# A feed-forward down projection computed by block products: seven 2x2 products in place of eight, with the sums of the activations formed one stage earlier

## The chip, the cores and the metric

One core of a Trainium2 chip runs the whole program. The metric is device time in microseconds (us), the median of several executions, lower being better. The engines are TensorE (PE; its weight loads are listed apart as PEld), VectorE (DVE), ScalarE (ACT), GpSimd (POOL) and SyncE (SP), whose queue issues all DMAs here.

## The reference, cut

One decoder layer over 1024 prompt tokens and 64 sample tokens (8 sequences of 8), width D = 1024, feed-forward width 3072. The change concerns the last third of it, the feed-forward block and the final norm:

```python
h = modulate(x, p['g_norm2'], sh2, sc2)
up = h @ p['w_up']                               # 1024 -> 6144
uc, new_ffn_conv = causal_dwconv(ffn_conv, up, p['ffn_conv_w'], p['ffn_conv_b'])
ua, ub = jnp.split(uc, 2, axis=-1)
x = x + gt2[:, None] * ((jax.nn.gelu(ua) * ub) @ p['w_down'])   # 3072 -> 1024
...
y = rmsnorm(x, g_final)
```

All inputs and outputs are float32. TensorE runs on rounded float32 ("fp32r"), so each product is made of three matmuls: high part by high part, high by low, low by high. Splitting a tile in two costs one ACT copy (high part) and one DVE subtraction (low part).

## The kernel before, in words

Channels lie on the 128 partitions, tokens along the free axis. Tokens come in two halves: half 0 holds the 64 sample tokens and 512 prompt tokens (576 columns, multiplied as two pieces of 288), half 1 holds 512 prompt tokens. `x2d` in DRAM holds the residual, `modT` the gates.

**The up stage** (`up`, L1458) already uses seven block products for eight. For each of 24 blocks of 256 output channels (12 steps `b`, two parts each: the gelu side, then the other) a `Quad` (L1296) makes 2x2 blocks of output: two output channel groups by two token halves, from K cut in two. The products are `p1`, `p5`, `p6`, `p2`, `p3`, `p7` of one Quad and `p4` of the one before, which `up` places behind `p1`. `prod` (L1236) makes each of four channel blocks by three matmuls; of kind "w" with two 288-column pieces (p1, p2, p4, p6), "e" with 512 columns (p3, p5), "p" with two pieces of 256 (p7). `Blocks` (L1253) loads four weight blocks, forms four sums (`sums`, on DVE), and `take` splits one into a ring of 3 pairs `wh`, `wl`. Raw blocks and sums share `WR` = 9 buffers (tag "wr"), copies of partial results 4 buffers (tag "cp").

`evac_up` (L1390) brings a block of output from PSUM to SBUF, `finish` (L1474) applies the convolution (`conv_up`: one ACT and two DVE instructions), the gelu, and in part 1 the product with the gelu side (L1490), and stores the result to `actd` in DRAM (L1489, L1491): six DMAs per step.

**The down stage** then closes the pools of the up stage and opens its own, loads half 0's 24 activation blocks through 3 staging buffers (`load_act`, L1494) and splits each. `down_a` (L1502) makes 4 strips (`strip`, L211) of 256 output channels for half 0: 24 blocks of K x 2 groups x 3 matmuls x 2 pieces. `down_b` (L1521) loads half 1 and makes the same for it, 24 x 8 x 3 products: 468 matmuls of 512 columns and, for the last six blocks of K in three of the strips, 216 of 256 columns, so that the first 256 tokens are finished while the others are still being multiplied. Each strip of half 1 ends in a residual update kept in SBUF, squares for the norm, and `final` (L1578), which makes the norm from matmuls with a matrix of ones (`rstd_from`, L353), a square root on ACT and a reciprocal on DVE (L368), and multiplies and stores `y`. `final` of half 0 runs under half 1's matmuls.

The order on each engine is set at build time by the framework's scheduler: instructions whose inputs are expected to be there go first by program order, and `tc.high_priority` moves some ahead. On the chip each queue then keeps that order. A tile of a pool with n buffers waits until the tile n places earlier is released.

Of the kernel before, what the change touches and what calls it, by code (L numbers as in the profile page):

```python
# [42 lines left out]
NOUT = _n  # L43
# [8 lines left out]
def _body(ctx, nc, tc, a):  # L52
# [36 lines left out]
    obuf = const.tile([128, NOUT], F32, name="obuf")  # L89
# [68 lines left out]
    def rg(name):  # L158
        return tmp("rg", [128, 604], name, bufs=5 if two else 7)
# [985 lines left out]
    WR = 9  # L1145
# [61 lines left out]
    def h2b(ST):  # L1207
# [23 lines left out]
        for j in range(4):  # L1231
            c = load("xc", 2 * j + 1, 3)
            V.tensor_sub(A[j], c, A[j])
            split_form(form("T4", j), A[j])

    def prod(acc, kind, wt, n, start=False, stop=False):  # L1236
        hi, lo = [x.rearrange("p (j c) -> p j c", c=128) for x in wt]
        for j in range(4):
            X = F[n, j]
            for i, (y, r) in enumerate(((hi, 0), (hi, 1), (lo, 0))):  # L1240
                f = dict(start=start and j + i == 0, stop=stop and j == 3 and i == 2, skip_group_check=True)
# [11 lines left out]
    class Blocks:  # L1253


        def __init__(self, w, own=()):
            self.w, self.t = w, dict(own)

        def load(self, *names):
            for n in names:  # L1260
                t = self.t.setdefault(n, None)
                if t is None:
                    t = self.t[n] = wt("wr", f"w{n}", F32, WR)
                nc.sync.dma_start(t, self.w[{"A11": 0, "A12": 1, "A21": 2, "A22": 3}[n]])

        def sums(self, eng):
            t = self.t
            t["S1"] = wt("wr", "S1", F32, WR)
            eng.tensor_add(t["S1"], t["A21"], t["A22"])
            t["S2"] = wt("wr", "S2", F32, WR)  # L1270
# [3 lines left out]
            t["S4"] = wt("wr", "S4", F32, WR)  # L1274
            eng.tensor_sub(t["S4"], t["A12"], t["S2"])

        def take(self, n):
            with tc.high_priority(offset=300):
                hi, lo = wt("wh", "wh", F32R, 3), wt("wl", "wl", F32R, 3)
# [6 lines left out]
    def blocks_of(w):  # L1286
        q = Blocks(w)
# [5 lines left out]
    def product(q, acc, kind, n, x, **f):  # L1293
        prod(acc, kind, q.take(n), x, **f)

    class Quad:  # L1296


        def __init__(self, q, evac):
            self.q, self.evac, self.p3_ = q, evac, None  # L1300
# [5 lines left out]
        def p1(self):  # L1306
            self.b = mm("b")
            product(self.q, self.b, "w", "A11", "B11", start=True, stop=True)
            self.t1 = tmp("cp", [128, 576], "t1", bufs=4)
            self.cp(halves(self.t1), self.b[:, :, :288])  # L1310

        def p2(self):
            a_ = mm("a")
            product(self.q, a_, "w", "A12", "B21", start=True, stop=True)
            self.evac(0, 0, a_[:, :, :288], halves(self.t1))

        def p3_first(self, e):
            self.e = e
            product(self.q, e, "e", "S4", "B22", start=True, stop=True)
            self.p3_ = tmp("cp", [128, 576], "p3", bufs=4)[:, :512]  # L1320
            self.cp(self.p3_, e)

        def p5_last(self):
            product(self.q, self.e, "e", "S1", "T1", stop=True)
# [490 lines left out]
```

## Time and profile before

| | |
|---|---|
| median of 3 runs | 1755.53 us (1755.03 to 1757.67) |
| the profiled execution | 1756.53 us |
| its span, first to last instruction | 1754.7 us |
| matmuls busy, share of the span | 97% |
| VectorE, ScalarE busy | 71%, 52% |
| last matmul of the up stage ends | 1432.5 us into the span |
| last matmul of the down stage ends | 1743.5 us into the span |

Times inside the execution are counted from the start of its span. An idle time in square brackets is that of the engine just before the instruction, with the instruction that ended it. Matmuls overlap, so a single one's duration is longer than its share of a run of them.

### The profile page before, as it was taken

The page shows a single profiled execution, that of the slowest core. Times are in us where ns is not written, and L with a number is a line of the kernel's source. Part 1 is how long each engine was busy: PE and PEld are TensorE (multiplying, and loading weights), DVE is VectorE, ACT ScalarE, POOL GpSimd, SP SyncE. Part 2 cuts the span into 40 slices and gives each one's busy share as a digit, 9 for nine tenths or more (in the row PEclk, how much of TensorE's full clock was granted, in tenths as well). Part 3 has the DMA queues.
Part 4 walks back from the last instruction along what each step waited for, and adds up shares of the span by engine and source line. Part 5 has one row for each costly group of instructions (what it writes and reads, how often), then busy time and mean ns, then how long its engine had stood idle before and what let it go on. Part 6 is the DMA issues. An engine that isn't in the chain of part 4 may idle for free.

```text
span 1754.7 us, 29379 instructions
## 1 busy us (share of the span) xinstructions
PE 1698.0 (97%) x10542; PEld 1531.1 (87%) x10542; DVE 1241.7 (71%) x2629; ACT 913.7 (52%) x1608; POOL 219.6 (13%) x488
## 2 busy tenths in 40 slices
PE   7999999999999999999997999999999979999997
PEld 3899999999997877888776999999999968999887
DVE  8878688967846788666759877777777755436426
ACT  4557758535535587744446555555555544224224
POOL 0012110100000001020021222222222220000000
PEclk9999999999999999999999999999999989999999
DMA  8275334366646655445672222222222238546634
GB/s 304 77 228 180 101 107 137 119 187 207 194 139 199 206 182 153 124 156 183 202 232 71 78 74 74 75 74 74 78 79 83 70 99 260 163 128 189 200 93 137
DMA packets 151826, 250.87 MB, mean 143 GB/s; under 512 B 34048, under 2 KB 43264, under 8 KB 151680
## 3 DMA queue, kind: packets, MB, share of 16 engines
q1 hardware_dynamic: 151680, 248.99, 45.6%
q8 instruction: 83, 1.36, 0.3%
q14 instruction: 63, 0.52, 0.1%
HBM read 205.20 MB, written 43.73 MB: 142 GB/s over the span
## 4 chain that ended last, share of the span: by engine, by line
PE 69%; DVE 5%; DMA 4%; ACT 2%; issue 1%; POOL 0%; SPq 0%; POOLq 0%; DVEq 0%; ACTq 0%
PE mm L226 16%; PE b L1248 13%; PE mm L224 12%; PE e L1244 7%; PE mm L1536 7%; PE a L1248 4%; PE b L1251 3%; DMA al<-act 2%; DMA xB<-x 1%; PE pv L787 1%; PE pg L961 1%; DVE wlo L179 1%; PE sada L274 1%; PE sada L273 1%; DMA tgb<-tg 0%
## 5 line engine op out<-in xcount | busy, mean ns | idle before, releaser
L179 DVE TENSOR_TENSOR wlo<-raw,whi 128x512 fp32r<-128x512 f32 x310 | 214.1, 691 | 208.1 <-ACT whi L178 178.7
L178 ACT ACTIVATE whi<-raw 128x512 fp32r<-128x512 f32 x310 | 194.4, 628 | 315.9 <-PE mm L224 107.7
L224 PE MATMUL mm<-h1A,whi 128*128 128x288 f32 x1024 | 183.3, 298 | 0.0
L226 PE MATMUL mm<-h1B,whi 128*128 128x512 f32 x512 | 159.9, 393 | 0.0
L224 PEld LDWEIGHTS mm<-h1A,whi 128*128 128x128 f32 x1024 | 151.3, 189 | 0.2
L1248 PE MATMUL b<-T,wh 128*128 128x288 f32 x768 | 134.8, 297 | 7.9 <-ACT gl L1482 6.1
L1248 PEld LDWEIGHTS b<-T,wh 128*128 128x128 f32 x768 | 115.3, 190 | 10.7 <-ACT gl L1482 6.3
L245 ACT ACTIVATE wh<-wA 128x512 fp32r<-128x512 f32 x94 | 59.2, 630 | 109.7 <-PE b L1248 42.6
L226 PEld LDWEIGHTS mm<-h1B,whi 128*128 128x128 f32 x512 | 95.6, 188 | 23.1
L224 PE MATMUL mm<-h1A,wlo 128*128 128x288 f32 x512 | 110.6, 297 | 2.0 <-DVE wlo L179 2.0
L226 PE MATMUL mm<-h1B,wlo 128*128 128x512 f32 x256 | 100.7, 393 | 0.7 <-DVE wlo L179 0.7
L224 PE MATMUL mm<-act,whi 128*128 128x288 f32 x512 | 91.9, 300 | 2.0 <-ACT act L1157 1.0
L1383 DVE SCALAR_TENSOR_TENSOR uc<-up,vec,uc 128x624 f32<-128x624 f32 (+1 forms) x96 | 76.0, 806 | 22.2 <-POOL up L1375 12.4
L1383 DVE SCALAR_TENSOR_TENSOR gl<-up,vec,gl 128x624 f32<-128x624 f32 (+1 forms) x96 | 75.9, 805 | 20.5 <-ACT gl L1381 15.0
L224 PEld LDWEIGHTS mm<-h1A,wlo 128*128 128x128 f32 x512 | 82.4, 189 | 2.3 <-DVE wlo L179 2.3
L246 DVE TENSOR_TENSOR wl<-wA,wh 128x512 fp32r<-128x512 f32 x94 | 64.9, 691 | 26.8 <-ACT wh L245 26.3
L1248 PE MATMUL b<-T,wl 128*128 128x288 f32 x384 | 82.7, 297 | 0.0
L1536 PE MATMUL mm<-act,whi 128*128 128x512 f32 (+1 forms) x304 | 82.7, 359 | 0.0
L224 PEld LDWEIGHTS mm<-act,whi 128*128 128x128 f32 x512 | 76.6, 191 | 3.7 <-DVE act L1158 2.1
L245 ACT ACTIVATE wh<-S 128x512 fp32r<-128x512 f32 x72 | 45.0, 625 | 58.7 <-PE b L1248 42.6
L224 PE MATMUL mm<-act,w 128*128 128x288 f32 x384 | 56.5, 302 | 12.7 <-ACT act L1157 11.4
L1248 PE MATMUL b<-B,wh 128*128 128x288 f32 x384 | 67.2, 296 | 0.0
(456 smaller groups left out, 4370.5 us busy)
## 6 DMA issues: line engine op xcount, KB each, us to landing
raw<-w_in SPq DMA_DIRECT2D x128, 256.0 KB, 2.8
raw<-w_down SPq DMA_DIRECT2D x105, 256.0 KB, 2.8
wA<-w_up SPq DMA_DIRECT2D x94, 256.0 KB, 2.7
raw<-w_ada SPq DMA_DIRECT2D x56, 256.0 KB, 3.1
act<-uc SPq DMA_DIRECT2D x48, 256.0 KB, 2.1
araw<-w_ada SPq DMA_DIRECT2D x20, 512.0 KB, 7.0
s5a<-s5d SPq DMA_DIRECT2D x16, 512.0 KB, 3.8
raw<-w_rgp SPq DMA_DIRECT2D x32, 256.0 KB, 2.7
```

The source lines that it names most:

```text
L178: S.activation(hi, raw, AF.Copy)
L179: V.tensor_sub(lo, raw, hi.bitcast(F32))
L224: T_.matmul(T[m][:, h, :288], y[:, k, c], x[:, r, h * 288:(h + 1) * 288], **f)
L226: T_.matmul(T[0][:, m, tok], y[:, k, c], x[:, r, tok], **f)
L245: S.activation(hi, src, AF.Copy)
L246: V.tensor_sub(lo, src, hi.bitcast(F32))
L273: T_.matmul(sa[:18], csr[:, kb], hi, start=kb == 0, stop=False)
L1244: T_.matmul(acc, w, x, **f)
L1248: T_.matmul(acc[:, h, :288], w, x[:, h * 288:(h + 1) * 288], **f)
L1251: T_.matmul(acc[:, h, o:o + 256], w, x[:, h * 256:(h + 1) * 256], **f)
L1383: V.scalar_tensor_tensor(dst, t[:, k:k + n], fw[:, k, m:m + 1], dst, op0=OP.mult, op1=OP.add)
L1536: T_.matmul(T[:, m, tok], y[:, k, c], act[kb][:, r, tok], start=kb + n == 0, stop=kb == 23 and n == 2, skip_group_check=True)
```

## The change

The down projection becomes 16 Quads: four passes `ch`, each over three of the twelve pairs of activation blocks, times four groups of 256 output channels. Each Quad makes seven products of three channel blocks (w_down blocks of 128x384). Both token halves are made together. The sum of a pass goes into the residual in DRAM (`x2d` is read and written in every pass; in the last pass the result stays in SBUF). The seven activation forms of a pair (B11, B21, B22 and the sums T1 to T4) are formed in `finish` and stored in DRAM, 84 blocks in all in place of 48; the down stage loads and splits each once, with 28 buffers for 21 forms of a pass. `final` runs for half 1 behind the last Quad's p7 and for half 0 behind its p4. The weight buffers "wr" (now 8) and "cp" (now 5, in the same pool) live through both stages and also stage the forms; "uc" has 4 buffers for 3, "cs" 3 for 2; `obuf` moves to another pool; in `up_lead` the first Quad's p5 comes before the second's p3.

```diff
-    obuf = const.tile([128, NOUT], F32, name="obuf")
+    obuf = ph.tile([128, NOUT], F32, name="obuf")
...
-        return tmp("rg", [128, 604], name, bufs=5 if two else 7)
+        return tmp("rg", [128, 604], name, bufs=3 if two else 7)
...
+    ORDER, WIDE = ("B11", "T1", "T2", "B21", "B22", "T3", "T4"), ("B11", "B21", "T2", "T4")
-    actd = [dp.tile([24, 128, WID[h]], F32, name=f"act{h}") for h in range(2)]
+    actd = {n: dp.tile([12, 128, 576 if n in WIDE else 512], F32, name=f"act{n}") for n in ORDER}
...
-    WR = 9
+    WR = 8
...
-        for j in range(4):
-            X = F[n, j]
+        for j, X in enumerate(forms):
...
+    def cpt(name):
+        return uw.tile([128, 576], F32, tag="cp", name=name, bufs=5)
...
+        Q[0].p5_last()
         Q[1].p3_first(e[:, 1])
-        for q in Q:
-            q.p5_last()
+        Q[1].p5_last()
...
-            u, g = tmp("xc", [128, 632], "uc", bufs=3), gl[i, half]
+            u, g = tmp("xc", [128, 632], "uc", bufs=4), gl[i, half]
             conv_up(t, m, u[:, :n])
             if half == 0:
-                c = tmp("cs", [128, 64], "cs", bufs=2)
+                c = gl["c", i] = tmp("cs", [128, 64], "cs", bufs=3)
                 G.tensor_mul(two4(s8(c)), useg(u), useg(g))
-                nc.sync.dma_start(actd[0][k][:, :64], c)
-            V.tensor_mul(u[:, :512], u[:, :512], g[:, :512])
-            nc.sync.dma_start(actd[half][k][:, 512 * half - 512:] if half else actd[0][k][:, 64:576], u[:, :512])
...
+            u = gl["u", i, half] = u[:, :512]
+            V.tensor_mul(u, u, g[:, :512])
+        if part == 0:
+            return
+        b = k // 2
+        x = [gl["u", i, h] for h in range(2)]
+        if i == 0:
+            t1 = gl["T1"] = gl[0, 1][:, :512]
+            V.tensor_sub(t1, x[1], x[0])
+            store("B11", b, x[0], gl["c", 0])
+            store("T1", b, t1)
+            return
+        t2, t3, t4 = gl[0, 0][:, :512], gl["u", 0, 1], gl[1, 0][:, :512]
+        V.tensor_sub(t2, x[1], gl["T1"])
+        V.tensor_sub(t3, x[1], t3)
+        V.tensor_sub(t4, x[0], t2)
+        c = tmp("cs", [128, 64], "cs", bufs=3)
+        G.tensor_sub(c, gl["c", 1], gl["c", 0])
+        store("B21", b, x[0], gl["c", 1])
+        store("B22", b, x[1])
+        store("T2", b, t2, gl["c", 0])
+        store("T3", b, t3)
+        store("T4", b, t4, c)
+
+    def store(n, b, x, c=None):
+        d = actd[n][b]
+        if c is None:
+            nc.sync.dma_start(d, x)
+            return
+        nc.sync.dma_start(d[:, 32:544], x)
+        for h in range(2):
+            nc.sync.dma_start(d[:, 544 * h:544 * h + 32], c[:, 32 * h:32 * h + 32])
...
+        def load(ch, names):
+            for n in names:
+                for p in range(3 * ch, 3 * ch + 3):
+                    w = 576 if n in WIDE else 512
+                    x = FD[n, p] = pp.tile([128, 2, 576], F32R, tag="act", name=f"{n}_{p}", bufs=28)[:, :, :w]
+                    t = cpt("f") if n in WIDE else wt("wr", "f", F32, WR)
+                    nc.sync.dma_start(t, actd[n][p])
+                    split_form(x, t)
...
+            def evac(i, half, y, z):
+                m = 2 * b + i
+                d = x2d[half][m * 128:(m + 1) * 128]
+                if ch < 3:
+                    x = tmp("xr", [128, 512], "xr", bufs=5)
...
+                nc.sync.dma_start(x, d)
+                with tc.high_priority(offset=400):
+                    if z is None:
+                        z = cpt("c21")
+                        S.activation(halves(z), y, AF.Copy)
+                    else:
+                        o = halves(z) if len(y.shape) == 3 else z
+                        V.tensor_add(o, y, o)
+                if half == 0:
+                    t = tmp("rs", [128, 64], "rs")
+                    G.tensor_mul(two4(s8(t)), sv(z), two4(bc(modT[:, 40 + m, 1:9], [128, 8, 8])))
+                    G.tensor_add(xs[:, m], xs[:, m], t)
+                    z = z[:, 32:544]
+                V.scalar_tensor_tensor(x, z, modT[:, 40 + m, 0:1], x, op0=OP.mult, op1=OP.add)
+                if ch < 3:
+                    nc.sync.dma_start(d, x)
+                elif b < 3:
+                    acc_sq(acc[half], x, m == 0)
+                    S.activation(x, x, AF.Copy, scale=v("gf")[:, m:m + 1])
+                else:
+                    last[half].append(rg("sq")[:, :512])
+                    S.activation(last[half][-1], x, AF.Square)
...
+        load(0, ORDER)
+        for ch in range(4):
+            for b in range(4):
+                q = Quad(blocks_of(a["w_down"][b, ch], 384), evac_down(ch, b),
+                         lambda n, ch=ch: [FD[n, p] for p in range(3 * ch, 3 * ch + 3)])
+                q.p1()
+                if pend is not None:
+                    pend.p4()
+                ahead = (lambda n: load(ch + 1, (n,))) if ch < 3 and b == 3 else lambda n: None
+                if ch < 3 and b == 2:
+                    load(ch + 1, ORDER[:2])
+                q.p5()
+                ahead("T2")
+                q.p6()
+                ahead("B21")
+                q.p2()
+                ahead("B22")
+                q.p3()
+                ahead("T3")
+                q.p7()
+                ahead("T4")
+                pend = q
+        final(1, acc[1], last[1], X3[1])
+        pend.p4()
+        final(0, acc[0], last[0], X3[0])
+
+    def final(half, acc3, sq, X):
+        r = rstd_from([acc3, *sq], 512, "rstdF", f"rstdF{half}")
+        gf = v("gf")
...
-    early.close()
     pairs.close()
...
-    wp, tp, ph = pool("w2", 2), pool("tmp2", 2), pool("part2")
     pp = pool("act")
+    tp = pool("tmp2", 2)
     two = True
-    down_a()
-    down_b()
+    down()
...
-    A["w_down"] = blocks(f("w_down")[0])
+    w = f("w_down")[0].reshape(4, 3, 2, 128, 4, 2, 128)
+    A["w_down"] = np.ascontiguousarray(w.transpose(4, 0, 5, 2, 3, 1, 6)).reshape(4, 4, 4, 128, 384)
```

## Rows read from the trace of the kernel before

**Rows 1.** The page's engine table: busy time, share of the span, instructions.

```profile
PE 1698.0 (97%) x10542; PEld 1531.1 (87%) x10542; DVE 1241.7 (71%) x2629; ACT 913.7 (52%) x1608; POOL 219.6 (13%) x488
```

**Rows 2.** Chain of work, one Quad of the up stage: start us, us, engine, line, count.

```profile
1215.39 6.40 PE b L1248 x48
1221.80 2.80 PE e L1244 x12
1224.59 3.20 PE b L1248 x24
1227.80 3.20 PE a L1248 x24
1230.99 2.79 PE e L1244 x12
1233.79 2.84 PE b L1251 x24
```

**Rows 3.** Timeline of PE: end of up, start of down, end of down.

```profile
1432.09 0.42 PE L1248 MATMUL b<-T,wl 128*128 128x288 f32 x2
1443.57 4.99 PE L224 MATMUL mm<-act,w 128*128 128x288 f32 x24 [11.06 <-ACT act L1157]
...
1743.22 0.28 PE L1536 MATMUL mm<-act,wlo 128*128 128x256 f32 x1
```

**Rows 4.** Busy us (count) of PE, PEld, DVE, ACT, POOL; PEclk, DMA share, GB/s.

```profile
1102.50:1145.00 42.50, 42.50 (x291) 40.35 (x290) 32.97 (x49) 21.79 (x34) 11.53 (x30) 1.00 0.25 77
...
1440.00:1450.00 10.00, 6.34 (x32) 5.79 (x32) 4.67 (x7) 4.92 (x9) 0.00 (x0) 0.66 0.84 278
...
1490.00:1500.00 10.00, 9.37 (x71) 9.16 (x70) 7.10 (x16) 5.25 (x9) 0.00 (x0) 1.00 0.93 299
...
1580.00:1600.00 20.00, 20.00 (x152) 20.00 (x152) 12.10 (x19) 10.63 (x19) 0.00 (x0) 1.00 0.77 242
```

**Rows 5.** Timeline of DVE, ACT and SP around a store in a step of up.

```profile
1272.16 0.68 DVE L1490 TENSOR_TENSOR uc<-uc,gl 128x512 f32<-128x512 f32 x1
...
1274.98 0.91 ACT L1381 ACTIVATE gl<-up,vec 128x624 f32<-128x624 f32 x1 [1.12 <-POOL up L1371]
...
1286.82 1.62 ACT L1381 ACTIVATE gl<-up,vec 128x624 f32<-128x624 f32 x2 [0.33 <-POOL up L1371]
...
1259.08 0.33 SPq L1489 DMA_DIRECT2D act<-cs  x1
```

**Rows 6.** Groups by line and shape, DVE in up: busy us, mean ns, idle before.

```profile
L246 DVE TENSOR_TENSOR wl<-wA,wh 128x512 fp32r<-128x512 f32 x64 | 43.9, 685 | 16.8 <-ACT wh L245 16.4
L1383 DVE SCALAR_TENSOR_TENSOR uc<-up,vec,uc 128x512 f32<-128x512 f32 x32 | 23.9, 746 | 0.6
L1405 DVE TENSOR_TENSOR up<-a,t 128x576 f32<-128x576 f32 x16 | 12.1, 758 | 19.7 <-PE a L1248 19.7
```

**Rows 7.** A tile's instructions: min/median/max ns of a 256-column split on DVE.

```profile
L246 DVE TENSOR_TENSOR gw<-e,gw x16: 410/418/428, 137.8 to 736.2; 128x256 fp32r<-128x256 f32 x16
```

**Rows 8.** Groups by line and shape, DVE in down.

```profile
L1158 DVE TENSOR_TENSOR act<-al,act 128x512 fp32r<-128x512 f32 x24 | 16.5, 690 | 14.6 <-ACT act L1157 14.4
L1158 DVE TENSOR_TENSOR act<-al,act 128x576 fp32r<-128x576 f32 x5 | 3.8, 759 | 4.6 <-ACT act L1157 4.6
L368 DVE RECIPROCAL rstdF<-sd 128x512 f32<-128x512 f32 x1 | 3.4, 3354 | 1.3 <-ACT sd L363 1.3
```

**Rows 9.** DMA totals of two stretches: 1440 to 1490, then 1480 to 1500.

```profile
DMA packets 6933, 13.35 MB, mean 267 GB/s; under 512 B 771, under 2 KB 771, under 8 KB 6929
...
DMA packets 3198, 5.97 MB, mean 299 GB/s; under 512 B 351, under 2 KB 351, under 8 KB 3197
```

**Rows 10.** Timeline: a norm's matmuls and square root, and DVE's last work.

```profile
902.17 1.98 PE L357 MATMUL prs<-sq,ones 128*128 128x512 f32 x4
...
904.19 0.69 ACT L363 ACTIVATE rstdB<-prs,epst 128x512 f32<-128x512 f32 x1
...
1748.60 2.77 DVE L1593 TENSOR_TENSOR x<-x,rstdF 128x256 f32<-128x256 f32 x8
```

More of the change, by code (lines that the diff above doesn't have):

```diff
@@ L1253, in _body, with __init__ @@
     class Blocks:
-        def __init__(self, w, own=()):
-            self.w, self.t = w, dict(own)
+        def __init__(self, w, own=(), n=512):
+            self.w, self.t, self.n = w, dict(own), n
         def load(self, *names):
@@ L1291, in blocks_of, with __init__, prod @@
         return q
-    def product(q, acc, kind, n, x, **f):
-        prod(acc, kind, q.take(n), x, **f)
     class Quad:
-        def __init__(self, q, evac):
-            self.q, self.evac, self.p3_ = q, evac, None
+        def __init__(self, q, evac, forms):
+            self.q, self.evac, self.F, self.p3_ = q, evac, forms, None
+        def prod(self, acc, kind, w, x, **f):
+            prod(acc, kind, self.q.take(w), self.F(x), **f)
         def cp(self, dst, src):
@@ L1307, in p1 @@
             self.b = mm("b")
-            product(self.q, self.b, "w", "A11", "B11", start=True, stop=True)
-            self.t1 = tmp("cp", [128, 576], "t1", bufs=4)
+            self.prod(self.b, "w", "A11", "B11", start=True, stop=True)
+            self.t1 = cpt("t1")
             self.cp(halves(self.t1), self.b[:, :, :288])
@@ L1313, in p2 @@
             a_ = mm("a")
-            product(self.q, a_, "w", "A12", "B21", start=True, stop=True)
-            self.evac(0, 0, a_[:, :, :288], halves(self.t1))
+            self.prod(a_, "w", "A12", "B21", start=True, stop=True)
+            self.evac(0, 0, a_[:, :, :288], self.t1)
         def p3_first(self, e):
             self.e = e
-            product(self.q, e, "e", "S4", "B22", start=True, stop=True)
-            self.p3_ = tmp("cp", [128, 576], "p3", bufs=4)[:, :512]
+            self.prod(e, "e", "S4", "B22", start=True, stop=True)
+            self.p3_ = cpt("p3")[:, :512]
             self.cp(self.p3_, e)
         def p5_last(self):
-            product(self.q, self.e, "e", "S1", "T1", stop=True)
+            self.prod(self.e, "e", "S1", "T1", stop=True)
         def c12(self):
@@ L1388, in useg, with up_forms @@
         return two4(seg(x, 546, 10)[:, :, :8])
+    def up_forms(n):
+        return [F[n, j] for j in range(4)]
     def evac_up(b, part, gl):
@@ L1396, in evac @@
             o = t[:, 32:544] if half else t[:, :576]
-            o = halves(o) if len(y.shape) == 3 else o
+            o, z, e = [halves(x) if len(y.shape) == 3 and x is not None else x for x in (o, z, e)]
             with tc.high_priority(offset=400):
@@ L1462, in up @@
             for part in range(2):
-                q = Quad(blocks_of(a["w_up"][12 * part + b]), evac_up(b, part, gl))
+                q = Quad(blocks_of(a["w_up"][12 * part + b]), evac_up(b, part, gl), up_forms)
                 q.p1()
```

159 lines of the change are left out of this document (41 added, 118 removed).

## The prediction, made before the changed kernel was run

> **What bounds the kernel now.** I read the page's engine table first: PE is busy for 97% of the span [rows 1], so what shortens the matmuls shortens the kernel, unless another engine or the DMAs take over. Then the chain of waits through the up stage, because it holds the very Quad that the change brings to the down stage. One Quad is six entries of PE with nothing between them [rows 2]: 6.40 + 2.80 + 3.20 + 3.20 + 2.79 + 2.84 = 21.23 us. So a Quad with four channel blocks per product can run at PE's pace, with DVE busy for 33.0 and ACT for 21.8 us of the 42.5 us of a step (two Quads) and DMA at 77 GB/s [rows 4]. Last, PE's timeline at the seams [rows 3]: the up stage's last matmul ends at 1432.5, the first of the down stage comes at 1443.6 after 11.06 us idle, the last ends at 1743.5, and the span at 1754.7. The down stage's matmuls thus lie in 311.0 us, and 11.2 us of norm and store follow.
>
> **Part 1, the products (removed and added).** Prices per matmul come from the runs in rows 2: 3.20/24 = 0.133 us for 288 columns, 2.80/12 = 0.233 for 512, 2.84/24 = 0.118 for 256. Before: half 0 has 24 x 8 x 3 x 2 = 1152 of 288 columns, 153.6 us; half 1 has 468 of 512, 109.2, and 216 of 256, 25.6. Sum 288.4 us. After: a Quad with three channel blocks costs 21.23 x 9/12 = 15.92 us, and 16 of them 254.8 us. **Gain 33.6 us**, all on the path. That is 11.6%, not the eighth that the count of products promises, because four of the seven carry the wider half of the tokens and p7 goes in pieces of 256.
>
> **Part 2, the seam between up and down.** Of the 311.0 us before, 311.0 - 288.4 = 22.6 us were lost, nearly all at the start: the 11.06 us until weights and activations arrive through newly opened pools, PE at its lower clock just after (granted clock 0.66 over 1440 to 1450, 24 matmuls in 4.99 us instead of 3.2), and a first strip that waits for each activation block [rows 3, 4]. After, the weight pool stays open, so the first Quad's weights are split before the up stage ends, and B11 can be staged early, since pass 0 needs only pairs stored long ago. But the forms take the place of the up stage's, and the four T4 tiles of up are read until its very last product. Right after it DVE has to finish the up stage (four convolution steps of 0.75, two products and three new sums of 0.69, about 6.5 us), and T2 and B21 stand behind that: p6 of the first Quad would like them 2.4 + 2.1 = 4.5 us after 1432.5. I price this at 9 us of lost PE, two or three waits and the lower clock after them. Bounds: 3 us if the splits find gaps, 17 us if each of B21, B22, T3 and T4 waits for a staging buffer (five "cp" buffers for 12 wide forms beside the Quad's own three). **Gain 13.6 us** (5.6 to 19.6).
>
> **Part 3, inside the down stage.** DVE: a split or sum of 384 columns lies between 0.418 for 256 [rows 7] and 0.685 for 512 [rows 6], so 0.55 us. A Quad has 7 splits and 4 sums (6.1), three additions from PSUM of at most 0.76 (2.1) and four residual updates of 0.746 (3.0): 11.2 us of 15.92. A pass adds 12 wide form splits of 0.759 and 9 of 0.690 [rows 8], 15.3 us: 60.1 of 63.7 us by durations, 94%. Eight instructions of 0.418 take 2.77 us [rows 7, 10], so each is worth some 0.07 less, and the pass comes to 53.5 us, 84%, as in a step of up with its new sums. But the forms bunch. Seven of the 28 buffers are free ahead; the other 14 forms can be split only while the last Quad of a pass gives up the old ones: 11.2 + 14 x 0.73 less the overlap is about 19 us of DVE in 15.9. The forms are due between 7 and 18 us into the next pass, so most of this is paid from slack. DMA: a pass moves 16 weight blocks of 197 KB, 5.9 MB of forms, and reads and writes 4.2 MB of residual each, 17.5 MB in 63.7 us. Over the first three passes, with the first and last pass's forms, it is 56 MB in 191 us, **293 GB/s**. Where queues were full the trace shows 267 and 299 GB/s [rows 9], and at 299 PE ran 9.4 of 10 us [rows 4]. At 299 the three passes are bound by PE, at 267 they take 210 us, 19 more. My terms for seam and passes, 9 + 9 = 18 us over 191, amount to the same as the lower rate, which is the row with the same mix of staged loads. So I take **3 us of stall at each of three changes of pass, loss 9 us** (0 to 27). ACT has less to do than DVE in every stretch of rows 4 and is given nothing of its own.
>
> On DMA size the Trainium skill speaks against the change ("DMA: Bandwidth & Descriptors", Bandwidth): it asks for at least 1 MiB per DMA for three quarters of the peak, and gives 138 GB/s at 64 KB and 341 at 1 MB. The new DMAs are 192 to 288 KB, so by interpolation, an estimate from that page, they would move well under 300 GB/s and the down stage would be bound by them. The trace disagrees in part: 288 KB and 256 KB loads with several in flight reach 299 GB/s [rows 9]. The same page (Specifications) gives some 358 GB/s as the limit of one core's HBM share; no run here holds that with blocks of this size.
>
> **Part 4, the end.** Before, the norm of the first 256 tokens of half 1 ran under matmuls, and 11.2 us follow the last one. After, both halves' norms stand behind the last Quad. From the end of p7: addition, update and square (2.5 us with hand-offs), a ones product of 1.0, square root 0.69 [rows 10], reciprocal 3.35 [rows 8] and eight products of about 0.61 make half 1 on DVE until 13 us. Half 0's update and square wait behind that (program order), then one ones product, root, reciprocal and products, 1.4 + 1.0 + 0.7 + 3.35 + 4.9 + 1.2 for the samples and 0.8 of hand-offs, and the 3.3 us that the last store took before: 30 us. Less p4 itself (2.4, counted in part 1) 27 us follow the matmuls. **Loss 15 us**. Bounds: 12 if half 0's update slips in before the first reciprocal, 20 if the sample norm comes in series.
>
> **Part 5, the up stage.** A step gets four DVE subtractions, 4 x 0.69 = 2.8 us: DVE 35.7 of 42.5. It issues 15 DMAs for 6, nine more of about 0.33 us on SP's queue [rows 5], which the weight loads share. Two things now wait: a weight load has one buffer less, and two of the four gl tiles are held until T2 and T4 have landed in DRAM. Behind the waiting ACT convolution (L1381) stand the weight splits, and PE behind these. But the first gl pair of a step takes the two tiles that are free by 1272.8, used at 1275.0, and the second pair is due at 1286.8, 14 us after the products [rows 5]. I take **loss 1 us** in all (0 to 6 within the forecast), mostly in the first Quads, where DVE is the limit.
>
> **Sum.** -33.6 - 13.6 + 9 + 15 + 1 = -22.2 us on a span of 1754.7: 1732.5. The profiled execution took 1.8 us more than its span and lay 1.0 above the median, so I predict **1733 us**.
>
> **The rivals.** (a) *The transfers decide.* One SP queue in fixed order issues everything; each load that waits for a staging buffer holds up those behind it. For: 56 MB in three passes need 293 GB/s. Against: 299 was held with PE running. At the 242 GB/s of 1580 to 1600 [rows 4] the passes take 231 us, 22 more than mine: 1755. From 245 GB/s down the kernel is slower than before; at 229 it is 1768. This is the case on the other side. The page's rule on size belongs here; by the rows alone it has 0.12. (b) *The up stage gives it back*: SP's queue, with stores that wait for sums in front of weight loads, costs 0.5 to 1 us for each of 22 Quads, 11 to 22 us: 1743 to 1755. Against: S1 to S4 are made about a Quad ahead. Chance 0.10. (c) *Seam and passes are hidden*: 3 us at the seam, none at the passes, 12 at the end: 1713 to 1722. Chance 0.15. (d) *It doesn't save what it says*, since padding eats the eighth: rows 2 exclude that, being the same products. Forecast, 1722 to 1745: 0.63.
>
> **How the numbers follow.** A measurement of this kernel tells about 0.2% (3.5 us) from no change, so 1752 and 1759 are the borders. (a) gives its 0.12 to slower with 0.10 and the rest to same, (b) mostly faster with 0.03 in same and 0.02 slower, the others are faster; with a little for what I did not see: faster 0.82, same 0.06, slower 0.12. The range from 1714 to 1756 leaves out the bottom of (c) and most of (a).
>
> **What would show it.** Right: Quads of 15.9 us on PE in the second and third column group of a pass; PE idle of 3 to 17 us after the up stage; DVE near 19 us in the last Quad of passes 0 to 2; 27 us behind the last matmul; a step of up still 42.5 us. Wrong: steps above 43 us (b), DMA share near 1 with PE waiting in the first Quads of every pass (a).

## The result, and the profile after

The changed kernel takes **1781.8 us**, the median of four runs (1778.3 to 1782.9), against 1755.9 us (1755.0 to 1757.7) before: ratio 1.0143 with a 95% interval of 1.0125 to 1.016. It is slower, by 25.9 us, where 1733 us and a gain were forecast. The profiled execution spans 1780.3 us.

The page's engine table, to be set against [rows 1], and one step (two Quads) of the up stage from the table of windows (columns as in [rows 4]):

```profile
PE 1682.0 (94%) x10432; PEld 1520.0 (85%) x10432; DVE 1372.9 (77%) x2835; ACT 959.0 (54%) x1706; POOL 276.7 (16%) x564
```

```profile
1002.50:1045.00 42.50, 42.50 (x291) 40.35 (x290) 35.12 (x53) 21.67 (x35) 13.74 (x32) 1.00 0.32 97
```

PE has less to do and more time in which it does nothing. The up stage is as it was: 42.50 us for a step, DVE at 35.1 (35.7 forecast). So the loss lies behind it. PE's timeline shows where: the end of the up stage, then every place in the first pass of the down stage, up to the first Quad of the second pass, where PE stood for over a microsecond; the square bracket is the idle time and who ended it.

```profile
1432.53 0.43 PE L1248 MATMUL b<-T,wl 128*128 128x288 f32 x2
1452.73 1.33 PE L1248 MATMUL b<-B,wh 128*128 128x288 f32 x4 [19.77 <-ACT wh L245]
...
1460.81 1.22 PE L1244 MATMUL e<-T,wh 128*128 128x512 f32 x2 [3.39 <-ACT wh L245]
...
1524.78 1.22 PE L1251 MATMUL b<-T,wh 128*128 128x256 f32 x4 [3.57 <-ACT u L1308]
...
1533.30 1.33 PE L1248 MATMUL b<-B,wh 128*128 128x288 f32 x4 [4.32 <-ACT wh L245]
```

The seam is 19.8 us of idle time where [rows 3] had 11.06. The last two lines stand for a pattern: ahead of p7 in the last Quad of a pass and ahead of p1 in the first Quad of the next, 3.57 and 4.32 us here, 3.22 and 4.77, 3.27 and 4.14 at the other two changes of pass. Behind each such wait four matmuls take 1.2 to 1.3 us, not 0.7, because the granted clock has fallen to 0.68 and 0.64 of full speed, so for some two thirds of the time to the lower of its two levels (1.2 of 2.4 GHz):

```profile
1520.00:1530.00 10.00, 5.42 (x24) 4.54 (x22) 5.25 (x8) 3.79 (x6) 0.94 (x2) 0.68 0.86 267
1530.00:1540.00 10.00, 6.68 (x35) 6.33 (x36) 9.76 (x19) 7.93 (x15) 0.00 (x0) 0.64 0.89 291
```

A count of all losses, worked out from the starts of each Quad's p1 in PE's timeline. A Quad in the middle of a pass takes 15.9 us (q5 from 1551.3 to 1567.2), as forecast; the first has no p4 of another to do and would take 13.5; the last, with its own p4 and the ones products of half 1, takes 21.4 (21.7 in no_reload below). So the **seam** is the time from the up stage's last matmul to the start of the third Quad, less 13.5 + 15.92 = 29.4; the **passes** are the time from there to the end of the last p4, less 13 x 15.92 + 21.4 = 228.4; the **end** is what follows. The cut lies at the third Quad because PE mixes the first two in most of the kernels below with forms loaded in place: in forms_in_place the second Quad's p1 starts at 1463.0 and the first one's p7 ends at 1468.4.

After: seam 1490.1 - 1432.97 - 29.4 = 27.7 us; passes 1757.88 - 1490.1 - 228.4 = 39.4; end 22.4, and 3.1 of the 21.4 (21.4 - 15.9 - 2.4 for p4) belong to it: 25.5.

| term, us | forecast | measured |
|---|---|---|
| products | -33.6 | -33.6 (16 x 15.92 against 288.4) |
| seam, from 22.6 | -13.6 | +5.1 |
| passes | +9 | +39.4 |
| end, from 11.2 | +15 | +14.3 |
| up stage | +1 | +0.5 |
| sum | -22.2 | +25.7 (the spans differ by 25.6) |

Two terms failed, seam and passes. What the trace says of each:

**The seam.** SP's queue (start, us, line, what it issues):

```profile
1443.20 0.64 SPq L1527 DMA_DIRECT2D actT<-cs  x1
1443.93 1.09 SPq L1556 DMA_DIRECT2D xr<-x2d  x2
1445.11 0.38 SPq L1542 DMA_DIRECT2D f<-actT  x1
1445.55 0.90 SPq L1542 DMA_DIRECT2D f<-actB  x2
1446.54 0.38 SPq L1542 DMA_DIRECT2D f<-actT  x1
1447.01 0.86 SPq L1264 DMA_DIRECT2D wA<-w_down  x2
```

The first Quad's weights (L1264) are asked for 14 us after the up stage's last matmul, behind that stage's last stores (L1527) and several forms (L1542).

**A change of pass.** ACT's timeline, in which u is the copy of the finished p6 out of PSUM, for which p7 waits:

```profile
1516.54 0.53 ACT L245 ACTIVATE wh<-wA 128x384 fp32r<-128x384 f32 x1 [1.41 <-PE b L1248]
1522.02 0.68 ACT L1158 ACTIVATE T<-f 128x576 fp32r<-128x576 f32 x1 [4.95 <-DMA f<-actT]
1523.56 0.68 ACT L1158 ACTIVATE T<-f 128x576 fp32r<-128x576 f32 x1 [0.85 <-DMA f<-actT]
1524.14 0.58 ACT L1308 ACTIVATE u<-b 128x512 f32<-128x512 f32 x1
...
1530.07 2.25 ACT L1158 ACTIVATE B<-f 128x576 fp32r<-128x576 f32 x4 [0.97 <-DMA f<-actB]
1532.22 0.61 ACT L1158 ACTIVATE T<-f 128x512 fp32r<-128x512 f32 x1
1532.74 0.92 ACT L245 ACTIVATE wh<-wA 128x384 fp32r<-128x384 f32 x2
```

p6 was done at 1516.5, but its copy stands in ACT's fixed order behind two T2 forms of the next pass, whose loads land at 1522; and the next Quad's first weight split (1532.74) stands behind the splits of B21 and B22. PE waits for forms that nobody needs yet. DMA moved 9.57 MB at 239 GB/s between 1505 and 1545, close to the 242 of rival (a). So two theories fit this trace: **Theory 1**, the forms hold buffers and places in the queues' order that the current Quad needs; **Theory 2**, the transfers are too slow, and everything waits for them.

### The profile page after: what moved, and what is told of

It is laid out like the page before. It is cut to its first block, busy times and chain, and to the rows that moved or that the text cites. A ratio compares the mean times of both kernels' runs of the same rounds, so it can differ in the third digit from the quotient of the medians.

```text
span 1780.3 us, 29893 instructions
## 1 busy us (share of the span) xinstructions
PE 1682.0 (94%) x10432; PEld 1520.0 (85%) x10432; DVE 1372.9 (77%) x2835; ACT 959.0 (54%) x1706; POOL 276.7 (16%) x564
## 4 chain that ended last, share of the span: by engine, by line
PE 68%; DVE 7%; DMA 3%; ACT 2%; issue 1%; SPq 0%; POOL 0%; DVEq 0%; ACTq 0%
PE b L1248 19%; PE mm L226 15%; PE e L1244 11%; PE mm L224 7%; PE a L1248 6%; PE b L1251 5%; DMA f<-actT 1%; DMA f<-actB 1%; PE pv L787 1%; PE pg L961 1%; PE sada L274 1%; DVE wlo L179 1%; PE sada L273 1%; DVE T L1159 0%; PE sx L717 0%
## 5 line engine op out<-in xcount | busy, mean ns | idle before, releaser
L1248 PEld LDWEIGHTS b<-T,wh 128*128 128x128 f32 x1152 | 174.7, 191 | 12.8 <-ACT gl L1489 6.4
L245 ACT ACTIVATE wh<-wA 128x512 fp32r<-128x512 f32 (+1 forms) x158 | 92.3, 586 | 149.6 <-PE b L1248 66.0
L246 DVE TENSOR_TENSOR wl<-wA,wh 128x512 fp32r<-128x512 f32 (+1 forms) x158 | 102.3, 649 | 59.7 <-ACT wh L245 59.0
L245 ACT ACTIVATE wh<-S 128x512 fp32r<-128x512 f32 (+1 forms) x120 | 70.3, 586 | 98.2 <-PE b L1248 48.6
L1248 PEld LDWEIGHTS b<-B,wh 128*128 128x128 f32 x576 | 89.6, 200 | 34.7 <-ACT wh L245 34.1
L1251 PE MATMUL b<-T,wh 128*128 128x256 f32 x576 | 95.3, 289 | 10.1 <-ACT u L1308 10.1
L1248 PE MATMUL a<-B,wh 128*128 128x288 f32 x576 | 100.7, 296 | 0.0
L246 DVE TENSOR_TENSOR wl<-S,wh 128x512 fp32r<-128x512 f32 (+1 forms) x120 | 76.2, 638 | 31.7 <-ACT wh L245 31.5
L1251 PEld LDWEIGHTS b<-T,wh 128*128 128x128 f32 x576 | 84.0, 196 | 14.6 <-ACT u L1308 11.4
L1244 PE MATMUL e<-T,wh 128*128 128x512 f32 x288 | 91.8, 400 | 4.4 <-ACT wh L245 3.4
L1248 PEld LDWEIGHTS b<-T,wl 128*128 128x128 f32 x576 | 93.8, 190 | 0.6 <-issue 0.5
```

The costliest lines, as they stand in the source:

```text
L245: S.activation(hi, src, AF.Copy)
L246: V.tensor_sub(lo, src, hi.bitcast(F32))
L1244: T_.matmul(acc, w, x, **f)
L1248: T_.matmul(acc[:, h, :288], w, x[:, h * 288:(h + 1) * 288], **f)
L1251: T_.matmul(acc[:, h, o:o + 256], w, x[:, h * 256:(h + 1) * 256], **f)
```

## The experiments

The table counts each kernel as above (us; a kernel measured twice has two lines). The times of the changed kernel, of the two lines with "again" and of the last three kernels are medians of four runs, the others single runs; the columns come from one profiled execution each. Kernels measured together ran on one chip with runs of the kernel before, whose median was 1755.9 to 1758.7; the up stage ended between 1432.1 and 1437.5 in these traces, so spans of different groups differ by some us, and the three columns are the safer measure. Where a kernel stands twice, its columns differ by up to 2.7 us; less than that is not read as an effect.

| kernel | time | seam | passes | end |
|---|---|---|---|---|
| changed kernel | 1781.8 | 27.7 | 39.4 | 22.4 |
| no_reload | 1742.3 | 27.6 | 0.3 | 22.5 |
| no_residual_traffic | 1767.2 | 25.3 | 23.3 | 22.4 |
| weights_first_at_seam | 1777.8 | 22.5 | 40.0 | 22.4 |
| forms_in_place | 1745.7 | 20.5 | 10.3 | 22.5 |
| narrow_in_place | 1775.5 | 23.1 | 37.0 | 22.5 |
| wide_in_place | 1758.2 | 27.3 | 12.4 | 22.5 |
| own_ring | 1761.2 | 34.3 | 8.1 | 22.4 |
| t4_later | 1784.6 | 27.8 | 39.8 | 22.7 |
| in_place_no_residual | 1736.3 | 19.7 | 1.0 | 22.5 |
| first_forms_staged | 1743.0 | 18.8 | 9.1 | 22.5 |
| the same again | 1745.8 | 19.3 | 11.7 | 22.5 |
| forms_in_place again | 1751.3 | 20.8 | 12.1 | 22.5 |
| last_stores_on_pool | 1746.2 | 15.4 | 15.2 | 22.8 |
| staged_b11_pool_end | 1749.2 | 19.7 | 11.8 | 24.0 |
| all_of_them | 1748.2 | 18.8 | 9.6 | 24.0 |

**What the changes of pass cost in all: no_reload.** `ahead` and the load at b == 2 are left out, and every pass reads `FD[n, 0..2]`.

> Leaves out the loads and splits of the forms of the second to fourth pass: those passes use the first pass's forms again, so their products are those of the wrong rows. It measures what the three pass changes cost altogether. Theory 1 and 2 alike: all Quads but the first run at 15.9-16.5 us and the time falls by 33-38 us to 1744-1749; what the other two edits leave of this tells which part of it is buffers and which bytes. If the changes cost only the 9 us of the forecast, the time would stay above 1770 and the loss would lie elsewhere.

Measured 1742.3 us: every Quad from q1 to q14 takes 15.9 us. The changes cost 39 us, all of it through the reload; the seam is untouched.

**Bytes: no_residual_traffic.**

```diff
-                nc.sync.dma_start(x, d)
+                if ch == 3:
+                    nc.sync.dma_start(x, d)
...
-                V.scalar_tensor_tensor(x, z, modT[:, 40 + m, 0:1], x, op0=OP.mult, op1=OP.add)
-                if ch < 3:
-                    nc.sync.dma_start(d, x)
+                V.scalar_tensor_tensor(x, z, modT[:, 40 + m, 0:1], z if ch < 3 else x, op0=OP.mult, op1=OP.add)
+                if ch < 3:
+                    pass
```

> Leaves out the reading and writing of the residual in the first three passes (2 MB of each Quad's transfers, 25 of the 56 MB that these passes move), so the residual that those passes add is lost; buffers, splits and order of the forms and weights stay. Theory 1: the changes keep their stalls, since the forms hold the same buffers; each change costs 9-12 us still and the time is 1768-1782. Theory 2 (transfers decide): each change falls to 3-5 us and the time to 1750-1758.

Measured 1767.2 us, a little below the first range and 9 above the second. With 25 of 56 MB gone each change still costs 7.5 to 8.0 us, and the passes 23.3 us instead of 39.4: the bytes matter, but more than half of the loss stays without them. Fewer bytes shorten the time that a form holds its buffer (the 288 KB loads landed in 3.2 to 3.3 us at the median between 1505 and 1545, where they took 3.4 to 4.9) but do not remove the waits.

**Buffers: forms_in_place.** The load goes into the second half of the form's own tile, ACT splits from there into the first half, DVE subtracts in place:

```diff
-                    t = cpt("f") if n in WIDE else wt("wr", "f", F32, WR)
+                    t = x[:, 1].bitcast(F32)
                     nc.sync.dma_start(t, actd[n][p])
                     split_form(x, t)
```

> Each product sum (form) is loaded into the second half of its own tile and split there, so that neither ring of staging buffers (the one of the weight blocks, the one of the copies t1, u2, p5, c21) is used by forms; the bytes, the splits and the order of the program stay. Theory 1 (forms stand ahead of the weights and the copies in shared rings and in the engines' fixed orders): the 7 us stalls of SP's queue at the three pass changes go, the last Quad of a pass falls from about 25.7 to 17-20 us and the first of the next from 18.5 to 16-17; each change costs 2-5 us instead of 12-13, and the time is about 1750-1758 against 1781.8. The seam keeps most of its loss if it is set by order on ACT and SP, and shrinks to 10-14 us if the ring alone held the weights. Theory 2 (transfers decide: the bytes of a change do not go through in its time): the same bytes, so the changes keep 10 us or more each and the time stays within 1772-1785.

Measured 1745.7 us, 36 less than the changed kernel and 10 less than the kernel before: the passes cost 10 us, not 39, with the same bytes, splits and program. Two slices of the first change of pass, from the table of windows of this kernel:

```profile
1510.00:1520.00 10.00, 8.86 (x62) 8.25 (x61) 9.85 (x17) 8.03 (x16) 1.06 (x2) 1.00 0.88 309
1520.00:1530.00 10.00, 10.00 (x64) 9.19 (x63) 9.89 (x18) 5.33 (x10) 1.32 (x2) 1.00 0.96 321
```

Here DMA moves 309 and 321 GB/s while PE is busy for 8.9 and 10 of 10 us. The DMA view's totals for 1505 to 1545, first of the changed kernel, then of this one:

```profile
DMA packets 5369, 9.57 MB, mean 239 GB/s; under 512 B 601, under 2 KB 1645, under 8 KB 5365
```

```profile
DMA packets 6777, 12.14 MB, mean 304 GB/s; under 512 B 753, under 2 KB 1905, under 8 KB 6774
```

The low rate of the changed kernel was, for the most part, the effect of the waits and not their cause. Theory 2 falls as the main cause at the changes of pass. The Trainium skill asks for DMAs of at least 1 MiB for three quarters of the peak ("DMA: Bandwidth & Descriptors", Bandwidth). The trace does not agree for several DMAs in flight: 304 GB/s were held for 40 us with DMAs of 192 to 288 KB, each landing 3.5 to 6.2 us (medians by kind) after its issue.

**Which ring: narrow_in_place and wide_in_place.** The narrow forms were staged among the weight blocks (eight buffers), the wide ones among the copies t1, u2, p5 and c21 (five buffers). narrow_in_place, and with the condition turned round wide_in_place:

```diff
-                    t = cpt("f") if n in WIDE else wt("wr", "f", F32, WR)
+                    if n not in WIDE:
+                        t = x[:, 1].bitcast(F32)
+                    else:
+                        t = cpt("f") if n in WIDE else wt("wr", "f", F32, WR)
```

> Only the narrow forms (B22, T1, T3: 512 columns, staged in the changed kernel in the ring of the weight blocks) are loaded into their own tiles; the wide ones (B11, B21, T2, T4) stay in the ring of the copies. Theory 1a (the ring shared with the weights is what costs): most of the 36 us that both together gave comes with this half alone: 1748-1756, the next Quad's weights arrive in time, and SP's 7 us waits are gone. Theory 1b (the ring of the copies costs, since ACT's copies t1, u2, p5 and c21 stand behind forms in it): little comes of it, 1770-1780. Theory 2 (transfers decide) is out after the run with both: same bytes, 305 to 274 us of down stage.

> The other half: the wide forms are loaded into their own tiles, the narrow ones stay in the ring of the weight blocks. Theory 1a (weights' ring): little gain, 1768-1780, and SP's waits of about 7 us for the sum's buffer stay. Theory 1b (copies' ring): most of the gain, 1748-1756, and the idle time ahead of the last Quads' p7 (3.2 to 3.6 us, behind ACT's u2 copy) goes while that ahead of the next p1 stays.

Measured 1775.5 us with the narrow forms in place and 1758.2 with the wide ones. This speaks against the weights' ring and for the copies' ring. The trace had pointed to the weights' ring: the longest single wait of SP's queue at each change (7.2, 8.1 and 7.3 us) is a form load that waits for a weight buffer. In narrow_in_place that wait is gone, and the change costs as much as before, at another place. ACT's and PE's timelines of narrow_in_place, where t is the copy of p1, done at 1523.0:

```profile
1529.01 0.63 ACT L1158 ACTIVATE B<-B 128x512 fp32r<-128x512 f32 x1 [2.07 <-DMA B<-actB]
1529.54 0.51 ACT L245 ACTIVATE wh<-S 128x384 fp32r<-128x384 f32 x1
1530.87 1.32 ACT L1158 ACTIVATE B<-B 128x512 fp32r<-128x512 f32 x2 [0.82 <-DMA B<-actB]
1532.10 0.67 ACT L1158 ACTIVATE T<-f 128x576 fp32r<-128x576 f32 x1
1533.75 1.31 ACT L1158 ACTIVATE T<-T 128x512 fp32r<-128x512 f32 x2 [0.98 <-DMA T<-actT]
1534.96 0.63 ACT L1308 ACTIVATE t<-b 128x576 f32<-128x576 f32 x1
```

```profile
1535.65 1.33 PE L1248 MATMUL b<-T,wh 128*128 128x288 f32 x4 [7.55 <-ACT t L1308]
```

The copy is made 12 us after its product, behind six form splits in these lines, and p6 of the new Quad, which adds to the same PSUM tile, waits 7.55 us. With the wide forms out of the copies' ring no such wait is left in the passes; none is longer than 1.3 us. The seam keeps all its loss in wide_in_place (24.1 us idle), and 4.6 us of it go with the narrow forms.

**Sharing or staging: own_ring.** The wide forms keep a staging buffer, but in a ring of their own with three buffers; for the room, the forms have 26 buffers, not 28.

```diff
-                    t = cpt("f") if n in WIDE else wt("wr", "f", F32, WR)
+                    t = tmp("ld", [128, 576], "f", bufs=3) if n in WIDE else wt("wr", "f", F32, WR)
```

> The wide forms are staged as in the changed kernel but in a ring of their own (three buffers), paid for by 26 instead of 28 buffers for the forms; the copies' ring has the copies alone. Theory 1b says that the sharing costs and not the staging: as with the wide forms loaded into their own tiles, 1753-1763. If the extra trip through a staging buffer is what costs (three buffers, each held from the issue until DVE's split is done): 1770-1782.

Measured 1761.2 us; the passes cost 8.1 us, as little as in the best kernels with all the bytes. So it is the sharing that costs, not the way through a staging buffer. The seam got worse (34.3). SP's queue shows that here the first B11 too are asked for behind the last stores (at 1447.5), and the first Quad's weights behind them, 19 us after the up stage's last matmul instead of 14.

**Order alone: t4_later.** The T4 forms are loaded a Quad later, ahead of p3 of the new pass's first Quad.

> The changed kernel with its staging rings, and one edit: the three T4 forms of the next pass are loaded not behind the last Quad's p7 but in the next pass's first Quad, ahead of its p3 (their own use, p4, comes one Quad later). In the changed kernel the first Quad's copy t1 takes a buffer of the copies' ring behind the T4 forms, and stands behind their splits in ACT's fixed order. Theory 1b (ring order and ACT's order put the copies behind forms that are not needed yet): the idle time ahead of the last Quad's p7 and the next p1 shrinks, each change costs 4-9 us instead of 12-13, and the time is 1756-1774. If the number of transfers and splits in the last Quad is what costs, only its share (3 of 15 forms, 2-3 us per change) goes: 1773-1777.

Measured 1784.6 us, outside both ranges: the passes cost 39.8 us as before. The T4 forms were not what stood ahead. In this kernel PE stops earlier, ahead of p7 behind the T2 forms (3.98 us) and ahead of the next p1 behind B21 and B22 (4.36 us), as in the changed kernel, and both places come before T4 is loaded. I had carried over the order seen in narrow_in_place to a kernel with another one.

**What is left when the rings are free: in_place_no_residual.** forms_in_place, and the residual's reading and writing of the first three passes left out as above.

> All forms loaded into their own tiles, and the reading and writing of the residual in the first three passes left out (25 MB of the 56 MB; what those passes add is lost). It asks what transfers still cost once the rings are out of the way. If nothing (the remaining 4-5 us of the first two changes are splitting work on DVE and ACT): 1741-1746, within 4 us of the 1745.7 with the residual. If the transfers hold the rest: the Quads around the changes fall to 15.9-16.3 us each and the time to 1731-1737.

Measured 1736.3 us, in the second range. The Quads around the changes fall to 15.9 to 16.7 us and the passes from 10.3 to 1.0. One slice of the first change, to be set against the first of forms_in_place above:

```profile
1510.00:1520.00 10.00, 10.00 (x70) 9.47 (x69) 9.79 (x18) 8.25 (x16) 1.20 (x2) 1.00 0.93 304
```

DVE is as full as there (9.79 of 10 us against 9.85), and PE does not stop. So DVE's work is not what forms_in_place still loses: nearly all of that, 9.3 us, belongs to the transfers of the residual or to their places in SP's queue; these two were not told apart.

**The seam: weights_first_at_seam, first_forms_staged, last_stores_on_pool.** In the first, the first Quad's `blocks_of` stands ahead of `load(0, ORDER)`, in the changed kernel. In the second, this is added to forms_in_place, with the three B11 of the first pass staged among the copies. In the third, forms_in_place issues the last pair's stores from POOL:

```diff
         d = actd[n][b]
+        e = nc.gpsimd if b == 11 else nc.sync
...
-        nc.sync.dma_start(d[:, 32:544], x)
+        e.dma_start(d[:, 32:544], x)
```

> The only edit: the first Quad's weight blocks and their sums stand in the program ahead of the 21 loads of the first pass's forms, not behind. Theory 1 (at the seam the weights arrive late because forms stand ahead of them in the ring and in SP's order): the first product of the down stage starts when its first form is there, about 8-11 us after the last product of the up stage instead of 19.8, and the time falls by 8-12 us to about 1770-1774; the pass changes stay as they are. Theory 2 (the seam waits for the transfers of the first forms behind the stores): the idle time stays at 17-20 us and the time at 1779-1784.

> All forms loaded into their own tiles but the three B11 of the first pass, which go through the copies' ring, and the first Quad's weights ahead of them in the program: these three loads can then be issued ahead of the up stage's last stores, where a load into a form's own tile stands behind them. If the seam of 14.9 us is held by these three loads alone: first product of the down stage 4-9 us after the up stage's last, and 1736-1741. If it is held by what follows (T1 and the others come behind the stores as before, and ACT's split waits for the up stage's last work): the first product earlier, but idle behind it, and 1743-1747.

> All forms loaded into their own tiles, and the stores of the up stage's last pair of rows are issued by POOL instead of SP, so that SP's queue reaches the down stage's first loads without waiting for DVE and POOL to finish that pair. Theory A (the seam is SP's fixed order: the first pass needs only rows stored long before, but its loads stand behind the last stores, issued at 1439.5-1443.3): the loads go out at about 1434-1437, the first product comes 6-10 us after the up stage's last instead of 14.9, and the time is 3-8 us below the run with forms in place. Theory B (the seam is DVE's and ACT's last work of the up stage, or the memory that the forms' tiles take over): the idle time stays at 12-15 us and the time within 3 us of that run.

weights_first_at_seam: 1777.8 us, less of a gain than expected. The first product comes 3.5 us after the up stage, but PE then stops again for 5.2 us (for DVE, which finishes the up stage), 2.4 and 4.3 us, and the seam falls by 5 us only. first_forms_staged: the same early start and the same stop for DVE, then one of 3.2 us, and a seam of 18.8 against 20.5 us, so its second expectation holds. last_stores_on_pool: the seam is 15.4 us against 20.8 for forms_in_place on the same chip. 3 of these 5.3 us come back in the passes (15.2 against 12.1), near the spread; the medians differ by 5.1 us (1746.2 against 1751.3), where the three columns differ by 2.0 in all. PE's first product and SP's queue in last_stores_on_pool:

```profile
1441.63 0.85 PE L1248 MATMUL b<-B,wh 128*128 128x288 f32 x2 [6.88 <-ACT B L1158]
```

```profile
1436.23 0.34 SPq L1675 DMA_DIRECT2D o_sfc<-vec  x1
1437.09 0.34 SPq L1676 DMA_DIRECT2D o_pfc<-fcarry  x1
1437.52 2.72 SPq L1543 DMA_DIRECT2D B<-actB  x3
```

The first forms are asked for 2.8 us after the up stage's last matmul (1434.7), where they stood behind the stores before, and the idle time falls from 15.05 to 6.88 us. So half of that idle time, and a quarter of the seam's loss, was SP's fixed order; the rest of the seam stays open. From 1440 to 1460 this kernel's DMA share is 0.94 and 1.00, at 309 and 388 GB/s, so the transfers may hold a part of that rest; no run tests it. The Trainium skill ("Perfetto Trace Analysis", DMA Optimizations) says that one engine for loads and another for stores may make sense, above all with loops or control flow. The trace agrees here: the seam is 5.3 us shorter.

**The end: staged_b11_pool_end, all_of_them.** first_forms_staged with eight of the last sixteen products on POOL; all_of_them has T4 later as well.

```diff
-                    V.tensor_mul(x, x, r)
+                    (G if half or b == 0 else V).tensor_mul(x, x, r)
```

> The run with the first B11 staged and all other forms in place, and at the end POOL makes the first six of the last products with the norm's factor for half 1 and two of those for half 0, so that DVE has eight fewer of 0.62 us behind the last matmul. Theory (the end is DVE's chain: two reciprocals of 3.35 us, sixteen products, the sample's norm): the 22.5 us behind the last product fall to 18-20 us and the time to 1738-1741. If POOL's products cost as much on DVE's side as they save (they slow each other, or POOL at 1.3-1.8 us each is late): 1742-1745.

> The run before with the T4 forms loaded one Quad later as well. With the rings out of the way, the order should matter little: the Quads around the changes lose 1 to 2 us less where SP's queue and the transfers were pressed, 1733-1740. If spreading the loads only moves the waits: the same time as the run before, within 3 us.

1749.2 and 1748.2 us (on a chip where the kernel before took 1758.2): the first is above both of its ranges, and the second within 3 us of the first, so T4 later did nothing once more. The end became longer, 24.0 us for 22.5; the last section looks at it.

**The comparison of the good ones.**

> The kernel with the first B11 staged and all other forms in place once more, beside the next one on the same chip: if its gain of 3 us over forms in place is real, its median is 2-4 us below; if that was the spread of single runs, within 1.5 us. Against the kernel before 10-14 us faster.

> The kernel with all forms in place once more. Theory 1 (rings) with the interval that one run could not give: 8-11 us faster than the kernel before, ratio 0.994-0.996; theory 2 (transfers) would have it at 1.01 or above as the changed kernel.

Four runs each, on one chip: forms_in_place 1751.3 us, ratio to the kernel before 0.9953 (0.9936 to 0.997); first_forms_staged 1745.8, 0.9928 (0.991 to 0.9947); last_stores_on_pool 1746.2, 0.9921 (0.9903 to 0.9939). So the seven products do make a faster kernel than the eight, by 0.5 to 0.8%, once the forms have buffers of their own. first_forms_staged was 5.5 us below forms_in_place, more than the 2 to 4 expected; seam and passes of the profiled executions account for 1.8 of that, and the rest is not explained.

## Why the prediction failed, step by step

- **Part 1, the products,** held to the tenth: 15.9 us a Quad. **Part 5, the up stage,** held as well (42.50 us a step, 0.5 us in all).
- **Part 4, the end,** came out at +14.3 us for +15, but two errors offset each other in it, so the closeness is in part luck. The sum had half 0's update, square, ones product and root wait behind the products of half 1, 3.1 us in a row. The update slipped in ahead of them, behind the first reciprocal, and the rest ran under them. The samples' norm took 2.9 us instead of 1.2. DVE's timeline (c is the copy for half 0):

```profile
1756.88 3.35 DVE L368 RECIPROCAL rstdF<-sd 128x512 f32<-128x512 f32 x1 [2.70 <-ACT sd L363]
1760.15 0.65 DVE L1569 SCALAR_TENSOR_TENSOR x<-c,modT,x 128x512 f32<-128x512 f32 x1
1760.72 3.69 DVE L1614 TENSOR_TENSOR x<-x,rstdF 128x512 f32<-128x512 f32 x6
```

- **Part 2, the seam,** failed at the sentence "the weight pool stays open, so the first Quad's weights are split before the up stage ends". The pool was open, but the weights' place in SP's queue was behind the last stores and the forms: asked for at 1447.0, split at 1452.2. I had asked whether there was room, and not what stood ahead in the queue. 27.7 us for 9; the upper bound of 17 had counted waits of forms for buffers, and none of the weights. This step alone is not all of the loss: with the weights ahead of the forms 5.2 us came back, with the forms in place 7.2, and with the last stores moved to POOL 5.3 more. 15.4 us are left even then, and why is open.
- **Part 3, the passes,** failed at the sentence "The forms are due between 7 and 18 us into the next pass, so most of this is paid from slack". A form that is due late still has a place in ACT's and SP's order and a buffer in the ring, and the current Quad's copies come behind it. Slack of the consumer is no slack for those queued behind. I had named the five "cp" buffers for 12 wide forms in part 2, for the seam, and not used them for the three changes, where the same 12 forms pass through the same ring. ACT was "given nothing of its own" because it has less to do than DVE; it was ACT's order that held PE, not its load. DVE was busy for 19.6 to 20.8 us in the last Quad of passes 0 to 2, near the 19 forecast, but these Quads took 25.6 to 26.4 us. 39.4 us for 9; what Part 3 weighed was DVE's work and the DMA rate, and neither was the main cause.
- **Rival (a)** gave the right direction. It even names the mechanism, loads that wait for a staging buffer and hold up those behind them in SP's queue, but prices it as a DMA rate. Its sign, a DMA share near 1 with PE waiting, nearly came true (0.86 and 0.89 in the windows above, 239 GB/s over the change), yet the same transfers run at 304 GB/s when the rings are free. Leaving out the residual's traffic gives 16.1 us in the passes with the shared rings and 9.3 with the rings free, so how much of the 39.4 us one calls transfers depends on the rings. Its border is off as well: by its own sum the kernel falls behind the one before from 242 GB/s down, not from 245. **Rivals (b) and (d)** fell with the unchanged step and the Quads of 15.9 us; **(c)** was reached by no kernel that does all the work.
- With the rings free, the forecast would have been short by 12.8 us: forms_in_place loses 20.5 + 10.3 us at seam and passes where 9 + 9 were put, and its 1745.7 us lies in the range.

## What to carry to other kernels

Before prefetching through a ring that another step uses, write down who takes the next buffers in program order, and what a copy that is needed at once has to wait for: an early load that is not needed yet can hold up a late copy that is. Load into the final tile and split in place where the tile has room for the raw data. When the DMA rate is low while PE waits, free the waits before calling the transfers the limit.

## What the hardware showed that I had not expected

DVE's products with two inputs in SBUF took about twice as long while POOL did the same kind of product. DVE and POOL at the end of staged_b11_pool_end (L1618 and L1620 are the products with the norm's factor):

```profile
1728.64 3.44 DVE L1620 SCALAR_TENSOR_TENSOR x<-x,vec,rstdF 128x512 f32<-128x512 f32 x2
1732.00 3.34 DVE L368 RECIPROCAL rstdF<-sd 128x512 f32<-128x512 f32 x1
1735.26 0.93 DVE L385 TENSOR_REDUCE accs<-sqs 128x64 f32<-128x512 f32 x1
1736.11 5.25 DVE L1618 TENSOR_TENSOR x<-x,rstdF 128x512 f32<-128x512 f32 x4
1741.28 1.40 DVE L1620 SCALAR_TENSOR_TENSOR x<-x,vec,rstdF 128x512 f32<-128x512 f32 x2
```

```profile
1728.30 11.91 POOL L1618 TENSOR_TENSOR x<-x,rstdF 128x512 f32<-128x512 f32 x8 [1.04 <-DVE rstdF L368]
```

While POOL works (1728.3 to 1740.2), two products (L1620) take DVE 3.44 us, 1.72 each; two of the same kind take 1.40 us once POOL is done. Four of the other kind take 5.25 us, 1.31 each, the last of them at least in part after POOL's end; in the changed kernel six take 3.69, 0.61 each. The reciprocal, with one input, keeps its 3.34. So eight products fewer gained DVE nothing: its last work ends 18.9 us behind the last p4, as in first_forms_staged again. The 1.5 us by which the end grew lie behind that, between the issue of the last store and the end (5.1 us for 3.5), with more data still on its way (1.66 MB from 1743.0 on, 1.08 there). The Trainium skill says of the slowing ("SBUF — State Buffer", SBUF: two separate sides): a port pair is shared by DVE and GpSimd as an exclusive lock, and a DVE instruction with two SBUF inputs contends for it with a GpSimd instruction that reads SBUF. The trace agrees: of these instructions only those with two inputs are slower.
